# Six steps of the next row between one shift row's sum and its transposes, and three empty steps ahead of the first attention

## The chip, the cores and the metric

The kernel runs on one NeuronCore of a Trainium2 chip; nothing is shared with other cores. The metric is device time in microseconds (us) of one execution; the time before is the median of 3 runs. One more execution was profiled, and all rows of the trace come from it. TensorE (PE, with its weight loads PEld) multiplies matrices, VectorE (DVE) and ScalarE (ACT) do elementwise work, GpSimd (POOL) some small work and DMA issues, and SyncE (SP) issues most DMAs.

## The reference

One decoder block on x of 512 tokens and width 2048, in float32. The modulation comes from c (a vector of 2048): six vectors of 2048, shift, scale and gate for each half. Cut to what the change touches:

```
mod = silu(c) @ w_ada + b_ada            # shift1, scale1, gate1, shift2, scale2, gate2
h = rms_norm(x, norm1_w) * (1 + scale1) + shift1
aq, ak, av, gq, gf, gi, gg = split(h @ w_in)          # 7 parts of 1024 columns
attn = dilated_attention(rope(rms_norm(aq)), rope(rms_norm(ak)), av)   # 8 heads of 128
ho = hgrn2(gq, gf, gi, lb)               # f = lb + (1 - lb) * sigmoid(gf); 8 heads, chunked recurrence
...                                      # norms, silu(gg) gate, w_out, gate1, residual
x = x + gate2 * (square(relu(h2 @ w_ff1)) @ w_ff2)
```

The three branches of the dilated attention are merged by the weights of one masked softmax, so the kernel computes for each head the scores of 512 tokens against 512, one softmax and one product with the values.

## The kernel before

**Precision.** Each projection is made of three matmuls on parts in fp32r: a value is split into hi (a cast on ScalarE, L39) and lo (a subtraction on VectorE, L40), and hi x hi, hi x lo and lo x hi are summed in PSUM. `tok_mm` (L194, matmuls L198 to L200) puts tokens on partitions, `ch_mm` (L202, L206 to L208) puts channels there. The four buffers of each split tile (`whi`, `wlo`) let the splits run up to four k ahead of the matmuls.

**A projection.** `project` (L368) makes 512 columns: 16 steps of k (128 rows of the weight each), 12 matmuls of 128x128 by 128x512 in each, into four PSUM banks. The projections follow in this order: hv0 (values of the first half of HGRN heads), q0, k0, v0 (the first attention), `hgrn_q(1)` (L558, here hq1) and hv1, then q1, k1, v1 and two gate projections. Behind each, ScalarE copies the four banks out (`evac` L406, and L564 in `hgrn_q`). The next projection uses the same four banks, so its first matmuls wait for these copies.

**Two generators beside it.** Behind each k's matmuls, `project` calls `tick()` once, which takes one step of the first generator in `tasks` (HGRN heads, then attention, and so on), and then `bg_step()` as often as the rate says (2.0 for hv0, 1.85 for the others), which takes one step of the first generator in `bgw`, the background work. A step runs to the next `yield`. So the place of a `yield` decides behind which k an instruction stands on TensorE. From L835 on TensorE's instructions keep the order in which the program writes them (`manual_schedule`); the order on the other engines and the DMA queues is made by the tile framework's planner from its own model of times and priorities. `tc.high_priority()` marks what is to go first: weight loads and splits, the copies out of banks, and, with an offset of 400, the attention's softmax chain.

**The background rows.** A modulation or shift vector is a product of one vector with a matrix, and is made on VectorE: `gemv` (L116) loads one row block of 128 x 512 in each of 16 steps (SP's queue, L123) and multiplies and adds it to one of two accumulators (L127, L129). `to_cols` (L138) adds the two accumulators (the sum, L143), yields, and then lets TensorE transpose the result in four parts into one bank (L149), from which ScalarE sums each part into a column (L152). `mod_cols` makes such columns for the modulation, and `mod_rows` (L172) collects four of them, waits 3 steps, transposes the whole column into a bank `pr` (L180) and stores it to DRAM as gate1.

**Shift rows.** The first HGRN projections are made from h without shift1, and the shift's part is added afterwards: `shift_through(col0)` (L748) is `gemv` with the shift vector, `to_cols`, and then, for 4096, the forget gates of heads 0 to 3 (`forget`, L554: sigmoid on ScalarE, L555, and VectorE, L556), for 3072 the queries (L755 to L758). Its 18 steps are 16 rows, the sum, and the transposes with all that follows. Ahead of hv0 the background takes 76 steps: 72 of the four `shift_gen` and the first 4 of `shift_through(4096)`.

**HGRN heads.** `hgrn` takes 12 steps for each of four heads; a step mixes VectorE's products (`level`, L591) with small matmuls (`blocks32`, L577).

**Attention.** `attention` (L444) works on four heads: `heads_t(h)` transposes queries and keys (two banks, copied out by ScalarE at L456), `scores(h)` makes four matmuls into three banks (L468) and the softmax chain: VectorE's scale and mask (L474), maximum (L476, L477), ScalarE's exponential (L478). Four steps later `weights_t(h)` transposes the weights (three banks, L490, copied at L492), then `heads_t(h + 1)`, and in one step `values(h)` (one bank `po`, L501, divided and written by VectorE at L505) and `scores(h + 1)`. It has 25 steps. It is appended to `tasks` behind v0, and hgrn for the second half behind hv1.

**PSUM.** There are eight banks: four tagged "mm" for the projections and four tagged "bg" that everything else takes in turn.

Of the kernel before, what the change touches and what calls it, by code (L numbers as in the profile page):

```python
# [18 lines left out]
NK = D // P  # L19
# [25 lines left out]
def hybrid_block(ctx, tc, x, c, positions, norm1_w, w_ada, b_ada, w_in, q_norm_w, k_norm_w,  # L45
# [22 lines left out]
    def bank(name, tag="bg"):  # L68
        return ps.tile([P, 512], F32, name=name, tag=tag)
# [46 lines left out]
    def gemv(view, vec, col0, n=512, early=False):  # L116

        accs = [(work("acc") if early else gv.tile([P, 512], F32, name="acc"))[:, 0:n] for _ in range(2)]
        nk = 512 // n
        for k0 in range(0, NK, nk):  # L120
            raw = spare.pop(0) if early and spare else slot("araw") if early else gv.tile([P, 512], F32, name="araw", bufs=4)
            raw = raw.rearrange("p (k n) -> p k n", n=n)
            nc.sync.dma_start(raw, view[:, k0:k0 + nk, col0:col0 + n])  # L123
            for k in range(k0, k0 + nk):
                acc = accs[k % 2]
                if k < 2:
                    dve.tensor_scalar(acc, raw[:, k - k0], vec[:, k:k + 1], None, op0=ALU.mult)  # L127
                else:
                    dve.scalar_tensor_tensor(acc, raw[:, k - k0], vec[:, k:k + 1], acc, op0=ALU.mult, op1=ALU.add)  # L129
            yield  # L130
        gemv.acc = accs
# [6 lines left out]
    def to_cols(accs, dst):  # L138

        nb = accs[0].shape[1] // P  # L140
        parts = 1 if nb == 4 else 2
        if parts == 1:
            dve.tensor_tensor(accs[0], accs[0], accs[1], op=ALU.add)  # L143
        yield
        pc = bank("pc")
        for j in range(nb):
            for u in range(parts):
                c = (j * parts + u) * P
                pe.transpose(pc[:, c:c + P], accs[u][:, j * P:(j + 1) * P], ident)  # L149
        for j in range(nb):  # L150
            c = pc[:, j * parts * P:(j + 1) * parts * P]
            act.activation(c, c, AF.Copy, accum_out=dst[:, j:j + 1])  # L152
# [78 lines left out]
    def work(name, dt=F32):  # L231
        return wk.tile([P, 512], dt, name=name, tag="wk")
# [55 lines left out]
    def first_groups(c_f, c_q, before, after):  # L288

        bt = [bank("prj", tag="mm") for _ in range(4)]  # L290
        bc = [bank("prc") for _ in range(2)]
        for k0 in range(0, NK, 2):
            before(k0)
            wt = load_w(win_v, k0, c_f, ahead=False)
            wc = load_w(win_v, k0, c_q, 256, None, ahead=False)
            for j in range(2):
                k = k0 + j
                ch_mm(bt, hhi[k], hlo[k], *wt[j], k == 0, k == NK - 1)
                ch_mm(bc, hhi[k], hlo[k], *wc[j], k == 0, k == NK - 1)
            after(k0)  # L300
        return bt, bc
# [42 lines left out]
    bgw = []  # L344
# [9 lines left out]
    tasks = []  # L354
# [83 lines left out]
    def qk(c0, name, i):  # L438
        ts = evac(project(c0, tok_mm), name)
        rs = sm.tile([P, NT, 4], F32, name=f"rs{i}", bufs=2)  # L440
        bgw.insert(0, qk_norm(ts, i, rs))
        return ts if i else (ts, rs)

    def attention(qr, ks, vs):  # L444
        qs, rsq = qr

        place = {3: (0, 0), 2: (1, 0), 0: (1, 384), 1: (2, 0)}

        def heads_t(h):
            tT = []  # L450
            for i, src in enumerate((qs, ks)):
                pt = bank("ptq")
                for ti in range(NT):
                    pe.transpose(pt[:, ti * P:(ti + 1) * P], src[ti][:, h * DH:(h + 1) * DH], ident)
                t = work("qT")
                act.activation(t, pt, AF.Copy, scale=wcol[:, i:i + 1])  # L456
                tT.append(t)
            return tT

        def scores(h, qT, kT):  # L460
            lsum = sm.tile([P, NT], F32, name="lsum")
            m = sm.tile([P, NT], F32, name="m")
            ps_s = [bank("pscore") for _ in range(3)]
            s_sb = [work("s_sb") for _ in range(3)]
            for ti in (3, 2, 0, 1):
                n = (ti + 1) * P
                b, o = place[ti]
                pe.matmul(ps_s[b][:, o:o + n], lhsT=qT[:, ti * P:(ti + 1) * P], rhs=kT[:, 0:n], start=True, stop=True)  # L468
            for ti in (3, 2, 0, 1):
                n = (ti + 1) * P  # L470
                b, o = place[ti]
                s = s_sb[b][:, o:o + n]
                with tc.high_priority(offset=400):
                    dve.scalar_tensor_tensor(s, ps_s[b][:, o:o + n], rsq[:, ti, h:h + 1], lnc_sb[:, 512 - n:512],  # L474
                                             op0=ALU.mult, op1=ALU.add)
                    dve.tensor_reduce(m[:, ti:ti + 1], s, axis=AX.X, op=ALU.max)  # L476
                    dve.tensor_scalar(m[:, ti:ti + 1], m[:, ti:ti + 1], -1.0, None, op0=ALU.mult)  # L477
                    act.activation(s, s, AF.Exp, bias=m[:, ti:ti + 1], accum_out=lsum[:, ti:ti + 1])  # L478
            return s_sb, lsum

        def weights_t(s_sb):
            p_sb = []
            for b, tis in enumerate(((3,), (2, 0), (1,))):
                pT = bank("pT")
                p_sb.append(work("p_sb"))
                for ti in tis:
                    o = place[ti][1]
                    for sj in range(ti + 1):
                        c = slice(o + sj * P, o + (sj + 1) * P)
                        pe.transpose(pT[:, c], s_sb[b][:, c], ident)  # L490
                n = 256 if b == 2 else 512
                act.copy(p_sb[b][:, 0:n], pT[:, 0:n])  # L492
            return p_sb

        def values(h, p_sb, lsum):
            hs = slice(h * DH, (h + 1) * DH)
            po = bank("po")
            for ti in range(NT):
                b, o = place[ti]
                for sj in range(ti + 1):  # L500
                    pe.matmul(po[:, ti * P:(ti + 1) * P], lhsT=p_sb[b][:, o + sj * P:o + (sj + 1) * P],  # L501
                              rhs=vs[sj][:, hs], start=sj == 0, stop=sj == ti)
            dve.reciprocal(lsum, lsum)
            for ti in range(NT):
                dve.tensor_scalar(qs[ti][:, hs], po[:, ti * P:(ti + 1) * P], lsum[:, ti:ti + 1], None, op0=ALU.mult)  # L505

        tT = heads_t(0)
        yield
        p_sb = None
        for h in range(4):  # L510
            if h:
                values(h - 1, p_sb, lsum)
            s_sb, lsum = scores(h, *tT)
            for _ in range(4):
                yield
            p_sb = weights_t(s_sb)
            yield
            if h < 3:
                tT = heads_t(h + 1)
                yield  # L520
        values(3, p_sb, lsum)
        yield
# [31 lines left out]
    def forget(hd, src, f, bias=0.0):  # L554
        act.activation(f, src, AF.Sigmoid, bias=bias)  # L555
        dve.tensor_scalar(f, f, omlb[:, hd:hd + 1], lb[:, hd:hd + 1], op0=ALU.mult, op1=ALU.add)  # L556
# [191 lines left out]
    def shift_through(col0):  # L748

        yield from gemv(win_v, s1c, col0, early=col0 < 4096 + 512)  # L750
        col = sm.tile([P, 8], F32, name="scol", bufs=2)
        yield from to_cols(gemv.acc, col[:, 0:4])
        for h in range(4):
            if col0 == 3072:
                dve.tensor_scalar(col[:, 4 + h:5 + h], col[:, h:h + 1], QS, None, op0=ALU.mult)  # L755
                sg = wk.tile([P, 512], F32, name="sg", tag="ev", bufs=2)
                act.activation(sg, hq0[h], AF.Sigmoid, scale=1.0 / QS, bias=col[:, h:h + 1])
                dve.scalar_tensor_tensor(hq0[h], hq0[h], col[:, 4 + h:5 + h], sg, op0=ALU.add, op1=ALU.mult)  # L758
            else:
                f, hd = ((f0, h), (f1, 4 + h))[(col0 - 4096) // 512]  # L760
                forget(hd, f[h], f[h], col[:, h:h + 1])
        yield

    bgw += [shift_through(4096), shift_through(3072)]
    bt, bc = first_groups(4096, 3072, scale_block, shift_start)
    f0 = keep(bt, "f")
    hq0 = keep(bc, "gq", QS)
# [74 lines left out]
    q0 = qk(0, "aq", 0)  # L842
    k0_ = qk(1024, "ak", 1)
    v0 = evac(project(2048, tok_mm), "av")
    tasks.append(attention(q0, k0_, v0))
    hq1 = hgrn_q(1)
    hv1 = evac(project(5120 + 512, tok_mm), "gi")
    tasks.append(hgrn(f1, hq1, hv1, hrs[1]))
# [576 lines left out]
```

## Time and profile before

| | |
|---|---|
| median of 3 runs | 2282.14 us (2280.93 to 2285.49) |
| the profiled execution's own time | 2284.35 us |
| its span, first to last instruction | 2282.1 us |
| mean granted clock of TensorE | 0.996 of full speed |
| busy: PE, DVE, ACT, POOL | 97%, 79%, 48%, 19% of the span |
| moved by DMA | 598.31 MB, mean 262 GB/s |

Matmuls are pipelined: one that is shown with 390 ns starts about 230 ns behind the one before it, so the pace is read from the starts. A row of a timeline gives the start, the duration, the engine, the line, the operation with its output and inputs, the shape, the count, and in brackets the idle time of the engine before it with what ended it. A row of the waits gives the total, how often, and the longest. The clock column of a window is the share of full speed that TensorE was granted in it. What ended a wait is inferred from the semaphores' events.

### The profile page before, as it was taken

What the parts mean: (1) busy time and instruction counts of PE and PEld (TensorE: products, weight loads), DVE (VectorE), ACT (ScalarE), POOL (GpSimd) and SP (SyncE); (2) the same over time, 40 slices, a digit from 0 to 9 for tenths busy, and PEclk for the clock granted to TensorE, in tenths of its full rate; (3) what the DMA queues carried; (4) which work ended last, traced back from release to release, by engine and by line L of the source; (5) the groups of instructions that cost most, each with busy time, mean ns of one, the idle gap of its engine ahead of it and who ended that gap; (6) DMA issues with size and microseconds to landing.
All of it is one profiled execution on the core that took longest, in us unless ns stands there. A gap on an engine that the chain in (4) does not pass through costs nothing.

```text
span 2282.1 us, 33105 instructions
## 1 busy us (share of the span) xinstructions
PE 2224.0 (97%) x11769; PEld 1824.9 (80%) x11769; DVE 1809.7 (79%) x2765; ACT 1097.6 (48%) x1950; POOL 443.4 (19%) x664
## 2 busy tenths in 40 slices
PE   4899999999999999999999999999999999999999
PEld 3787877878778888888888888888888888888887
DVE  6999778668786575678658988988897679967878
ACT  5555344443444554547544555555564333443332
POOL 1000022000220000002232323323232222222221
PEclk9999999999999999999999999999999999999999
DMA  9799465546555256747979789889889987998884
GB/s 319 256 329 326 118 192 167 180 153 213 180 163 179 71 189 219 265 131 247 341 258 369 269 330 363 296 297 381 310 293 378 365 304 261 349 355 306 303 297 164
DMA packets 262582, 598.31 MB, mean 262 GB/s; under 512 B 23220, under 2 KB 43968, under 8 KB 262416
## 3 DMA queue, kind: packets, MB, share of 16 engines
q1 hardware_dynamic: 186800, 332.54, 43.3%
q0 software_dynamic: 70720, 254.21, 30.2%
q10 hardware_dynamic: 4896, 9.44, 1.2%
q8 instruction: 93, 1.52, 0.3%
q14 instruction: 73, 0.60, 0.1%
HBM read 518.49 MB, written 77.61 MB: 261 GB/s over the span
## 4 chain that ended last, share of the span: by engine, by line
PE 69%; issue 11%; DMA 11%; DVE 5%; POOL 3%; ACT 1%; SPq 0%; POOLq 0%; DVEq 0%; ACTq 0%
PE prj L198 9%; PE f L1183 9%; PE f L1182 9%; PE f L1181 9%; PE prj L200 9%; PE prj L199 9%; DMA f_lod<-fs 3%; PE f L208 2%; PE f L207 2%; PE f L206 2%; DMA araw<-in_w_ada_dram 2%; DMA araw<-in_w_in_dram 1%; DMA Fl<-f_lod 1%; DMA f_hid<-part 1%; PE prj L207 1%
## 5 line engine op out<-in xcount | busy, mean ns | idle before, releaser
L1165 ACT CAST vhi<-raw 128x1024 fp32r<-128x1024 f32 x392 | 413.4, 1055 | 533.9 <-PE f L1183 420.2
L1166 DVE TENSOR_TENSOR vlo<-raw,vhi 128x1024 fp32r<-128x1024 f32 x392 | 475.9, 1219 | 151.3 <-ACT vhi L1165 150.6
L1182 PE MATMUL f<-vlo,Fh 128*128 128x512 f32 x1376 | 537.0, 390 | 3.4 <-DVE vlo L1166 3.3
L1183 PE MATMUL f<-vhi,Fl 128*128 128x512 f32 x1376 | 535.7, 389 | 0.7 <-DMA Fl<-f_lod 0.7
L1181 PE MATMUL f<-vhi,Fh 128*128 128x512 f32 x1376 | 536.0, 390 | 0.0
L39 ACT CAST whi<-wraw 128x512 fp32r<-128x512 f32 (+1 forms) x368 | 220.0, 601 | 447.5 <-PE prj L200 309.2
L198 PE MATMUL prj<-whi,hi 128*128 128x512 f32 x896 | 365.1, 407 | 3.8 <-ACT gq L564 2.4
L200 PE MATMUL prj<-whi,lo 128*128 128x512 f32 x896 | 351.8, 393 | 0.0
L199 PE MATMUL prj<-wlo,hi 128*128 128x512 f32 x896 | 350.8, 392 | 0.0
L40 DVE TENSOR_TENSOR wlo<-wraw,whi 128x512 fp32r<-128x512 f32 (+1 forms) x368 | 242.4, 663 | 125.8 <-ACT whi L39 120.6
L129 DVE SCALAR_TENSOR_TENSOR acc<-araw,sc,acc 128x512 f32<-128x512 f32 (+1 forms) x392 | 253.2, 671 | 91.1 <-DMA araw<-in_w_ada_dram 90.0
L1182 PEld LDWEIGHTS f<-vlo,Fh 128*128 128x128 f32 x1376 | 258.3, 188 | 61.6 <-DVE vlo L1166 8.7
L1183 PEld LDWEIGHTS f<-vhi,Fl 128*128 128x128 f32 x1376 | 258.4, 188 | 55.0 <-DMA Fl<-f_lod 1.6
L1181 PEld LDWEIGHTS f<-vhi,Fh 128*128 128x128 f32 x1376 | 258.4, 188 | 53.4
L1149 DVE TENSOR_TENSOR raw<-raw,raw 128x1024 f32<-128x1024 f32 x224 | 268.0, 1217 | 3.3 <-DMA raw<-in_w_ff_dram 2.9
L198 PEld LDWEIGHTS prj<-whi,hi 128*128 128x128 f32 x896 | 169.3, 189 | 39.9 <-ACT gq L564 3.6
L200 PEld LDWEIGHTS prj<-whi,lo 128*128 128x128 f32 x896 | 168.9, 188 | 37.0 <-DVE lo L240 0.3
L199 PEld LDWEIGHTS prj<-wlo,hi 128*128 128x128 f32 x896 | 169.5, 189 | 32.4 <-DVE wlo L40 0.4
L1127 POOL DMA_DIRECT2D Fh<-f_hid x112 | 79.0, 705 | 425.8 <-PE f L1183 413.4
L208 PE MATMUL f<-hi,wlo 128*128 128x512 f32 x256 | 99.9, 390 | 1.9 <-DVE wlo L40 1.9
L206 PE MATMUL f<-hi,whi 128*128 128x512 f32 x256 | 100.3, 392 | 0.0
L207 PE MATMUL f<-lo,whi 128*128 128x512 f32 x256 | 99.6, 389 | 0.0
(311 smaller groups left out, 2913.1 us busy)
## 6 DMA issues: line engine op xcount, KB each, us to landing
raw<-in_w_ff_dram SPq DMA_DIRECT2D x224, 512.0 KB, 9.8
araw<-in_w_ada_dram SPq DMA_DIRECT2D x384, 256.0 KB, 4.3
Fh<-f_hid POOLq DMA_DIRECT2D x112, 512.0 KB, 6.7
Fl<-f_lod POOLq DMA_DIRECT2D x112, 512.0 KB, 7.9
wraw<-in_w_in_dram SPq DMA_DIRECT2D x104, 512.0 KB, 3.9
Fh<-h_hid POOLq DMA_DIRECT2D x60, 512.0 KB, 6.3
Fl<-h_lod POOLq DMA_DIRECT2D x60, 512.0 KB, 7.2
f_hid<-part POOLq DMA_DIRECT2D x48, 512.0 KB, 8.0
```

Of the source, the lines that this page charges most:

```text
L39: nc.scalar.copy(hi, src)
L40: (eng or nc.vector).tensor_tensor(lo, src, hi.bitcast(F32), op=ALU.subtract)
L129: dve.scalar_tensor_tensor(acc, raw[:, k - k0], vec[:, k:k + 1], acc, op0=ALU.mult, op1=ALU.add)
L198: pe.matmul(banks[ti], lhsT=hi[:, ts], rhs=whi, start=first, stop=False)
L199: pe.matmul(banks[ti], lhsT=hi[:, ts], rhs=wlo, start=False, stop=False)
L200: pe.matmul(banks[ti], lhsT=lo[:, ts], rhs=whi, start=False, stop=last)
L1149: dve.tensor_tensor(dst, a, b, op=ALU.subtract)
L1165: cast_done.append(act.copy(hi, src))
L1166: split_done.append(dve.tensor_tensor(lo, src, hi.bitcast(F32), op=ALU.subtract))
L1181: pe.matmul(banks[t], lhsT=fh[u][a][:, ts], rhs=whi[:, a], start=first, stop=False)
L1182: pe.matmul(banks[t], lhsT=fh[u][a][:, ts], rhs=wlo[:, a], start=False, stop=False)
L1183: pe.matmul(banks[t], lhsT=fl[u][a][:, ts], rhs=whi[:, a], start=False, stop=end)
```

## The change

Two things. The two shift rows 4096 (row a) and 3072 (row b) are no longer run one behind the other: `staggered` runs row a through its 16 rows and its sum (`NK + 1` steps), then six steps of row b, then what is left of a (its transposes and the forget gates), then the rest of b. The number of steps is the same. And `attention` gets an argument `lead`, the number of steps at its beginning in which it does nothing; the first attention gets 3, the second keeps 0.

```
-    def attention(qr, ks, vs):
+    def attention(qr, ks, vs, lead=0):
         qs, rsq = qr
...
+        for _ in range(lead):
+            yield
         tT = heads_t(0)
         yield
...
-    bgw += [shift_through(4096), shift_through(3072)]
+    def staggered(a, b, n_a, n_b):
+        for g, n in ((a, n_a), (b, n_b)):
+            for _ in range(n):
+                next(g)
+                yield
+        yield from a
+        yield from b
+
+    bgw.append(staggered(shift_through(4096), shift_through(3072), NK + 1, 6))
...
-    tasks.append(attention(q0, k0_, v0))
+    tasks.append(attention(q0, k0_, v0, 3))
```

## The prediction

> **What bounds the kernel now.** I read the page first, then the waits of TensorE, then the engines' timelines around the two places that the diff touches, then the windows of those places.
>
> ```profile
> span 2282.1 us, 33105 instructions
> ...
> PE 2224.0 (97%) x11769; PEld 1824.9 (80%) x11769; DVE 1809.7 (79%) x2765; ACT 1097.6 (48%) x1950; POOL 443.4 (19%) x664
> ```
>
> TensorE sets the time: it is busy 97% of the span. An edit that adds and removes no work can gain only what TensorE loses in waits, and what it loses by running slowly behind them. Its list of waits (who <- for what: us in all, times, longest) has three rows that matter here:
>
> ```profile
> PE pc L149 <- DVE acc L143: 4.8, 1, 4.8
> ...
> PE prj L198 <- ACT gq L564: 2.4, 2, 2.0
> ...
> PE prj L198 <- ACT gg L705: 1.3, 1, 1.3
> ```
>
> The first is the shift row's: the transposes of L149 wait once for the sum of L143. The second is at the seam between hgrn_q(1) and the projection behind it, under the first attention. The third is a seam under the second attention, which the diff leaves alone. TensorE's timeline (start, us, what, in brackets the idle time before it) shows the first:
>
> ```profile
> 207.57 0.39 PE L200 MATMUL prj<-whi,lo 128*128 128x512 f32 x1
> ...
> 210.29 0.39 PE L200 MATMUL prj<-whi,lo 128*128 128x512 f32 x1
> 215.53 1.12 PE L149 MATMUL pc<-ident,acc 128*128 128x128 f32 x4 [4.85 <-DVE acc L143]
> 216.30 0.78 PE L198 MATMUL prj<-whi,hi 128*128 128x512 f32 x1
> ...
> 220.29 0.47 PE L198 MATMUL prj<-whi,hi 128*128 128x512 f32 x1
> ...
> 242.87 0.60 PE L149 MATMUL pc<-ident,acc 128*128 128x128 f32 x4
> ```
>
> From 207.57 to 210.29 twelve matmuls start: 0.227 us from start to start, 2.72 us for the twelve of one k. TensorE would have started its transposes at 210.29 + 0.23 = 210.52 and did so at 215.53. Behind them nine matmuls, 216.30 to 220.29, take 0.443 each. The windows (length, busy us by engine, granted clock, DMA share, GB/s) tell why:
>
> ```profile
> 195.00:210.50 15.50, 15.50 (x72) 12.65 (x70) 14.86 (x25) 9.28 (x21) 0.53 (x1) 1.00 1.04 382
> 210.50:215.50 5.00, 0.18 (x1) 0.00 (x0) 5.00 (x10) 0.62 (x1) 0.00 (x0) 0.81 1.05 387
> 215.50:220.30 4.80, 4.77 (x14) 3.91 (x15) 4.41 (x8) 3.55 (x10) 0.00 (x0) 0.50 1.05 387
> 220.30:240.00 19.70, 19.70 (x88) 16.30 (x87) 15.16 (x27) 5.85 (x12) 0.00 (x0) 1.00 0.49 147
> ...
> 473.60:476.40 2.80, 2.80 (x7) 2.12 (x8) 1.46 (x4) 2.80 (x7) 0.00 (x0) 0.50 0.00 0
> ```
>
> The granted clock falls to 0.50 behind the wait and is 1.00 again at 220.3. So a wait of TensorE costs more than its own length. The seam, in the same timeline:
>
> ```profile
> 469.80 0.39 PE L208 MATMUL prj<-hi,wlo 128*128 128x512 f32 x1
> 472.14 0.50 PE L198 MATMUL prj<-whi,hi 128*128 128x512 f32 x1 [1.95 <-ACT gq L564]
> ...
> 473.60 0.79 PE L198 MATMUL prj<-whi,hi 128*128 128x512 f32 x1 [0.49 <-ACT gq L564]
> ...
> 476.33 0.46 PE L198 MATMUL prj<-whi,hi 128*128 128x512 f32 x1
> ```
>
> And ScalarE's side of it:
>
> ```profile
> 470.80 0.72 ACT L478 ACTIVATE s_sb<-s_sb,m 128x512 f32<-128x512 f32 x1 [2.90 <-DVE m L477]
> ...
> 471.53 0.56 ACT L564 COPY gq<-prj 128x512 f32<-128x512 f32 x1
> ...
> 475.46 0.58 ACT L564 COPY gq<-prj 128x512 f32<-128x512 f32 x1
> ```
>
> The copies that empty hgrn_q(1)'s four banks (L564) stand in ScalarE's queue behind an exponential of the attention, which waits 2.90 us for VectorE's maximum. The first copy starts 1.5 us after the last bank was filled (469.80 + 0.23), and exponentials stand between the four.
>
> **The change, part by part.** No instruction is added or removed.
>
> *The shift row.* In hv0's projection two background steps follow each k. Row a (4096) has taken 4 steps before it, so its 17th (the sum) and its 18th (transposes) both fall behind k 6. With six steps of row b between them the transposes fall behind k 9. Moved with them are 4 accumulating copies and 4 sigmoids on ScalarE and 4 operations of forget on VectorE. The rows' DMAs keep their order on SP (a's sixteen, then b's sixteen), since sum and transposes issue none; POOL's queue has nothing of either. Without the wait TensorE runs k 7 to 9 from 210.52 and reaches the transposes at 210.52 + 3 x 2.72 = 218.7. VectorE's rows:
>
> ```profile
> 211.13 0.68 DVE L40 TENSOR_TENSOR wlo<-wraw,whi 128x512 fp32r<-128x512 f32 x1
> ...
> 214.20 0.68 DVE L40 TENSOR_TENSOR wlo<-wraw,whi 128x512 fp32r<-128x512 f32 x1
> 214.80 0.68 DVE L143 TENSOR_TENSOR acc<-acc 128x512 f32<-128x512 f32 x1
> 215.40 0.68 DVE L40 TENSOR_TENSOR wlo<-wraw,whi 128x512 fp32r<-128x512 f32 x1
> ...
> 223.88 0.54 DVE L556 TENSOR_SCALAR f<-f,omlb,lb 128x512 f32<-128x512 f32 x1
> ...
> 225.00 0.69 DVE L40 TENSOR_TENSOR wlo<-wraw,whi 128x512 fp32r<-128x512 f32 x1
> ...
> 232.79 0.68 DVE L143 TENSOR_TENSOR acc<-acc 128x512 f32<-128x512 f32 x1
> ```
>
> The sum ends at 215.48, 3.2 us ahead of 218.7. What is late next? The three wlo of 211.13, 214.20 and 215.40 are those of k 8, 9 and 10 (whi has four buffers, so the cast of k+4 waits for the matmuls of k). TensorE needs them at 213.2, 216.0 and 219.1, and they end at 211.81, 214.88 and 216.08: all in time, the tightest by 1.1 us. The next one (225.00, k 11) would be 3.8 us too late for 221.9, but its cast stood behind the wait itself, as ScalarE's rows say:
>
> ```profile
> 221.81 0.60 ACT L39 CAST whi<-wraw 128x512 fp32r<-128x512 f32 x1
> 224.02 0.62 ACT L39 CAST whi<-wraw 128x512 fp32r<-128x512 f32 x1 [1.61 <-PE prj L200]
> ```
>
> These casts wait for TensorE, not for a transfer; k 7 now ends at 213.2, and the cast of k 11 can run then. The forgets end at 224.42, 8.9 us behind the transposes' start; from 218.7 that is 227.6, and row b's transposes, at hv0's end, now come at 242.87 - 7.3 = 235.6. Even the later sum of the timeline, 232.79, ends 2.1 us ahead of that. So this wait goes whole. Its worth needs the pace of four transposes without a wait, from a later stretch of TensorE's timeline:
>
> ```profile
> 352.24 0.66 PE L149 MATMUL pc<-ident,acc 128*128 128x128 f32 x4
> 352.65 0.47 PE L198 MATMUL prj<-whi,hi 128*128 128x512 f32 x1
> ```
>
> They take 0.41. From 210.52 the transposes and nine matmuls need 0.41 + 9 x 0.227 = 2.45 and would end at 212.97; they ended at 220.29. Gain 7.3.
>
> *The empty steps.* hgrn(0) has 48 steps and uses the 48 ticks of q0, k0 and v0, so the attention's first step falls behind k 0 of hgrn_q(1). Counted from there, the third head's scores fall behind k 13, and their exponentials on the seam. Three ticks later they fall behind k 0 of the next projection, which needs all four banks emptied; so they can't stand ahead of the copies any more. Around the seam stand instead the second head's weights_t (behind k 14) and the third's heads_t (behind k 15): copies that wait for TensorE alone, no VectorE chain. heads_t's eight transposes now lie between the last matmul of the one projection and the first of the next, and give the copies time. No DMA is in the attention, and its end, behind k 8 of hv1, moves to k 11 with four empty ticks left, so nothing behind it moves. Without the wait the nine matmuls from 472.14 on would start at 470.03 and be through at 470.03 + 9 x 0.227 = 472.07, not 476.33. Gain 4.3.
>
> *A new wait.* Counting on, the second head's values and scores now fall behind k 10, and in the same k the background transposes gate1's column (pr, L180), which stood alone there before. po and the scores take all four background banks, so pr must have po's, and TensorE's queue stands until VectorE's L505 has read it; behind it wait the matmuls of k 11. The nearest pairs, TensorE's scores and VectorE's L505:
>
> ```profile
> 438.77 2.32 PE L468 MATMUL pscore<-qT 128*128 128x512 f32 x8
> ...
> 462.38 2.32 PE L468 MATMUL pscore<-qT 128*128 128x512 f32 x8
> ```
>
> ```profile
> 438.97 1.13 DVE L505 TENSOR_SCALAR aq<-po,lsum 128x128 f32<-128x128 f32 x4 [1.11 <-PE po L501]
> ...
> 464.04 1.12 DVE L505 TENSOR_SCALAR aq<-po,lsum 128x128 f32<-128x128 f32 x4
> ```
>
> L505 ends 1.0 ahead of the scores' end in the first and 0.5 behind it in the second. So the cost is 0 (no gain is possible in a new wait) to 0.5; if VectorE's queue happens to stand at a row that has not landed, up to 5.1:
>
> ```profile
> DVE acc L129 <- DMA araw<-in_w_ada_dram: 90.0, 74, 5.1
> ```
>
> I take 0.5, from the nearest row. SP's store of the gate row waits as much longer, and the row loads behind it; they feed only background work.
>
> *Sum.* 7.3 + 4.3 - 0.5 = 11.1. The profiled execution took 2284.35 (span 2282.1 and 2.25 around it), so 2273.25 on its scale. It lies 2.21 above the median of the runs, so I predict 2282.14 - 11.1 = **2271.0**.
>
> **One rule on the clock.** The row 473.60:476.40 has the clock at 0.50 behind a wait of 1.95 and one of 0.49. [...]
>
> **The rivals.**
> *A wlo behind the forgets.* VectorE works its queue in order. The cast of k 13 is released by k 9's end, the very moment of the new transposes; if its wlo is queued behind the four forgets, as 225.00 is behind 223.88, it ends 225.69 - 215.53 = 10.2 behind the transposes' start, and TensorE wants it after 0.41 + 3 x 2.72 = 8.6. That is a wait of 1.6 and, at the seam's rate (4.3 for 2.4 of waiting), 1.8 of slow clock: 2274.4. For it: that order stands in the trace. Against: weight splits have high priority. 12%.
> *The seam keeps a wait.* Other ScalarE work (weights_t, heads_t, the tanh of gq) holds the copies as long: 2271.0 + 4.3 = 2275.3. For it: ScalarE is busy 2.80 of 2.80 in 473.60:476.40. Against: none of it waits for VectorE ahead of the copies. 12%.
> *The transfers are the bound.* From 195.0 to 220.3 the DMA share is 1.04 to 1.05 at 382 to 387 GB/s. If weights come no earlier, TensorE waits for them instead, the first gain is lost: 2271.0 + 7.3 = 2278.3, within 0.2%. Against: the casts' waits end on TensorE, and from 220.3 the share is 0.49. 5%. [...]
> *Slower: a re-made order of VectorE in q0 to v0.* All engines but TensorE are ordered anew by the planner from the diff on. hgrn's ladder alternates TensorE and VectorE at every tick; if VectorE starts it with the backlog of later forgets, a rung comes late. Each such wait, at the seam's size, costs 4.3. Two give 2279.6, three 2283.9, and from four on it is slower: 2288.2. Against it, VectorE waits for TensorE in the ladder, not the reverse:
>
> ```profile
> 256.40 0.29 DVE L618 TENSOR_TENSOR mt<-pA,hgm 128x128 f32<-128x128 f32 x1 [1.57 <-PE pA L577]
> ```
>
> Two or three 9%, four or more 8%.
> That the change doesn't do what it says would need the planner to move TensorE's instructions; it keeps their written order here, so that has no share of its own.
>
> **How the numbers follow.** The forecast has 54%. 0.2% is 4.6 us, about what a measurement can tell. Faster by more: forecast, first and second rival, 78%. Within: transfers 5% and two or three late rungs 9%, 14%. Slower: 8%. Range: below, the new wait at 0 (2270.5), the runs' spread of 1.2 under their median, and the 1.3 of the second attention's seam if a new order happens to take it: 2268.0. Above, up to the transfers' case: 2278.5. That holds 83%.
>
> **What would show it.** Right: the L143 row gone from TensorE's waits, or under 1 us; no half clock near 215; L564 gone from them; the matmuls at the seam 0.227 apart; pr behind the scores with at most 0.5 of idle. Wrong: a wait for wlo (L40) in hv0, a wait for gq or qT at the seam, waits at L577, or a DMA as releaser of a cast. The prediction falls if TensorE's waits between 200 and 500 still come to more than 3 us in all.

## The result, and the profile after

| | before | after |
|---|---|---|
| median of 5 runs each, one chip | 2282.23 us (2280.93 to 2287.92) | 2274.34 us (2274.03 to 2275.7) |
| ratio after to before, 95% interval | | 0.996 (0.9949 to 0.9972) |
| the profiled execution's own time | 2284.35 us | 2275.3 us |
| its span | 2282.1 us | 2273.6 us |

The change makes the kernel faster by 7.9 us in the medians, and by 6.4 to 11.6 us by the interval of the ratio; the forecast was 11.1 us, from 2282.14 to 2271.0. The measured time lies inside the forecast range of 2268.0 to 2278.5. Ratios use the runs within 1.5% of a kernel's fastest, and one run in all lies outside that, of e8_both_leads with 5777.86 us. The busy row of the page of after:

```profile
PE 2222.2 (98%) x11769; PEld 1824.7 (80%) x11769; DVE 1809.1 (80%) x2765; ACT 1096.9 (48%) x1950; POOL 442.2 (19%) x664
```

The counts behind the five engines are those of before: the work is the same, and the span is 8.5 us shorter. TensorE's list of waits, cut to 200 to 500 us:

```profile
PE pr L180 <- DVE aq L505: 2.3, 1, 2.3
PE pc L149 <- DVE acc L143: 0.3, 1, 0.3
```

Before, this stretch held 4.8 for L143 and 2.4 for gq. The first is down to 0.3, the second is gone (the copies stand at L566 now, two lines further down), and a wait of 2.3 at pr is new. TensorE's timeline at the shift row and at row b's transposes:

```profile
218.00 0.39 PE L200 MATMUL prj<-whi,lo 128*128 128x512 f32 x1
218.23 0.60 PE L149 MATMUL pc<-ident,acc 128*128 128x128 f32 x4
218.58 0.48 PE L198 MATMUL prj<-whi,hi 128*128 128x512 f32 x1
...
235.47 0.66 PE L149 MATMUL pc<-ident,acc 128*128 128x128 f32 x4 [0.28 <-DVE acc L143]
```

Row a's transposes follow the matmul before them at its pace. The windows of the stage:

```profile
210.00:220.00 10.00, 10.00 (x47) 8.28 (x47) 10.00 (x18) 3.39 (x9) 0.00 (x0) 1.00 1.05 387
```

TensorE is busy for 10.00 of 10.00 us at full clock, where before it stood for 4.85 us and then ran at 0.50. VectorE's timeline of the stage (the forgets stand at L558 now):

```profile
214.34 0.68 DVE L143 TENSOR_TENSOR acc<-acc 128x512 f32<-128x512 f32 x1
...
219.80 0.68 DVE L40 TENSOR_TENSOR wlo<-wraw,whi 128x512 fp32r<-128x512 f32 x1
...
221.80 0.55 DVE L558 TENSOR_SCALAR f<-f,omlb,lb 128x512 f32<-128x512 f32 x1
...
225.68 0.68 DVE L40 TENSOR_TENSOR wlo<-wraw,whi 128x512 fp32r<-128x512 f32 x1
...
234.73 0.68 DVE L143 TENSOR_TENSOR acc<-acc 128x512 f32<-128x512 f32 x1
```

The sum of row a ends at 215.02, 3.2 us ahead of the transposes. Row b's sum ends at 235.41, and that is the 0.28. At the seam behind hgrn_q(1), TensorE and then ScalarE:

```profile
460.88 0.40 PE L208 MATMUL prj<-hi,wlo 128*128 128x512 f32 x1
461.12 0.60 PE L454 MATMUL ptq<-ident,aq 128*128 128x128 f32 x4
461.56 0.60 PE L454 MATMUL ptq<-ident,ak 128*128 128x128 f32 x4
461.91 0.48 PE L198 MATMUL prj<-whi,hi 128*128 128x512 f32 x1
```

```profile
459.24 0.59 ACT L566 COPY gq<-prj 128x512 f32<-128x512 f32 x1
...
460.39 1.06 ACT L566 COPY gq<-prj 128x512 f32<-128x512 f32 x2
...
462.39 0.59 ACT L566 COPY gq<-prj 128x512 f32<-128x512 f32 x1
...
471.49 0.72 ACT L478 ACTIVATE s_sb<-s_sb,m 128x512 f32<-128x512 f32 x1 [5.81 <-DVE m L477]
```

The third head's queries and keys (eight transposes, L454) lie between the projections, no matmul waits for the copies, and the exponential that stood among them comes 9 us behind the last of them. Now the new wait, TensorE first:

```profile
437.80 2.39 PE L501 MATMUL po<-av,p_sb 128*128 128x128 f32 x20
440.03 2.32 PE L468 MATMUL pscore<-qT 128*128 128x512 f32 x8
444.62 0.28 PE L180 MATMUL pr<-ident,gcol 128*16 128x128 f32 x1 [2.27 <-DVE aq L505]
```

```profile
442.77 0.75 DVE L129 SCALAR_TENSOR_TENSOR acc<-araw,sc,acc 128x512 f32<-128x512 f32 x1 [1.47 <-DMA araw<-in_w_ada_dram]
443.44 1.12 DVE L505 TENSOR_SCALAR aq<-po,lsum 128x128 f32<-128x128 f32 x4
```

VectorE had nothing to do for 1.47 us, though po was filled: at the head of its queue stood a background row (L129) that had not landed, and the division of po (L505) stood behind it. The chain that ended last, in order of time, says the same from the other end:

```profile
438.12 4.55 DMA araw<-in_w_ada_dram
...
442.77 0.63 DVE acc L129
...
443.44 0.61 DVE aq L505 x3
...
444.62 0.28 PE pr L180
```

A load that serves only background work is on the path here, because two queues lie between it and the matmuls, and each was worked in order here: VectorE's, idle for 1.47 us ahead of the row with L505 behind it, and TensorE's, idle for 2.27 us at pr with k 11 behind it.

### The profile page after: what moved, and what is told of

Read it like the earlier page. It is cut to its first block, busy times and chain, and to the rows that moved or that the text cites. A ratio compares the mean times of both kernels' runs of the same rounds, so it can differ in the third digit from the quotient of the medians.

```text
span 2273.6 us, 33111 instructions
## 1 busy us (share of the span) xinstructions
PE 2222.2 (98%) x11769; PEld 1824.7 (80%) x11769; DVE 1809.1 (80%) x2765; ACT 1096.9 (48%) x1950; POOL 442.2 (19%) x664
## 4 chain that ended last, share of the span: by engine, by line
PE 76%; DVE 8%; DMA 7%; issue 6%; ACT 2%; POOL 1%; SPq 0%; POOLq 0%; DVEq 0%; ACTq 0%
PE f L1192 10%; PE f L1193 10%; PE f L1191 10%; PE prj L198 9%; PE prj L200 9%; PE prj L199 9%; DVE vlo L1176 2%; PE f L208 2%; PE f L206 2%; PE f L207 2%; PE prj L206 2%; PE prj L207 2%; PE prj L208 2%; DVE raw L1159 2%; DMA f_lod<-fs 1%
## 5 line engine op out<-in xcount | busy, mean ns | idle before, releaser
L198 PE MATMUL prj<-whi,hi 128*128 128x512 f32 x896 | 363.6, 406 | 1.3 <-ACT gg L707 1.3
L129 DVE SCALAR_TENSOR_TENSOR acc<-araw,sc,acc 128x512 f32<-128x512 f32 (+1 forms) x392 | 253.8, 673 | 98.6 <-DMA araw<-in_w_ada_dram 97.7
L198 PEld LDWEIGHTS prj<-whi,hi 128*128 128x128 f32 x896 | 168.3, 188 | 36.2 <-ACT gg L707 1.6
```

Source lines behind the costliest of these rows:

```text
L198: pe.matmul(banks[ti], lhsT=hi[:, ts], rhs=whi, start=first, stop=False)
```

## The experiments

Ratios are to the kernel before, run beside it on the same chip. The traces are compared at three anchors of TensorE's timeline, which are the same matmul in each kernel; a difference between two anchors is the worth of what lies between them, free of how the beginning went. They are the first `pA` of hgrn(0), hq1's first matmul, and one L198 behind hv1's end; in before and in after, anchor by anchor:

```profile
248.87 0.46 PE L577 MATMUL pA<-gq,kk 128*32 128x32 f32 x32
...
409.55 0.47 PE L206 MATMUL prj<-hi,whi 128*128 128x512 f32 x1
...
528.02 0.39 PE L198 MATMUL prj<-whi,hi 128*128 128x512 f32 x1
```

```profile
241.53 0.46 PE L579 MATMUL pA<-gq,kk 128*32 128x32 f32 x32
...
402.21 0.47 PE L206 MATMUL prj<-hi,whi 128*128 128x512 f32 x1
...
520.06 0.39 PE L198 MATMUL prj<-whi,hi 128*128 128x512 f32 x1
```

After is 7.34 ahead at the first two and 7.96 at the third. Of the 7.34, 0.38 is there already at hv0's first matmul (188.76 in before, 188.38 in after). So row a gave about 7.0, and seam and pr together only 0.6. The theory from here on: the seam is worth what was forecast, and pr's wait takes it back, because a row that has not landed stands at the head of VectorE's queue. Rivals: the seam was never worth 4; or pr waits for something else than that row.

### Each part alone

**e1_steps_only**: the six steps without the empty ones.

```
-    tasks.append(attention(q0, k0_, v0, 3))
+    tasks.append(attention(q0, k0_, v0))
```

> The six steps of row b alone, no empty steps. Theory (three waits that add up: row a's sum 7.3, the seam 4.3, pr behind the scores -4.3): row a's wait is gone, the seam's wait of about 2.4 with its slow clock stays, pr stands alone and waits for nothing; 2282.2 - 7.3 = 2274.9, so as fast as the whole change. Rival (the shortfall is spread over a re-made order, not one wait): the gain differs from 7.3 by more than 1.5, and small waits are found elsewhere.

Measured: 2278.41 us (2274.64 to 2279.36, 6 runs) beside 2284.75 (17 runs), ratio 0.9969 (0.9956 to 0.9981), 7.1 us by the ratio. The seam's wait is there as before, pr's is not; TensorE's waits between 200 and 800:

```profile
PE prj L198 <- ACT gq L566: 2.7, 2, 2.5
PE pc L149 <- DVE acc L143: 0.3, 1, 0.3
```

The first part does by itself what was forecast for it, and the new wait belongs to the second.

**e2_lead_only**: the empty steps without the six.

```
-    bgw.append(staggered(shift_through(4096), shift_through(3072), NK + 1, 6))
+    bgw += [shift_through(4096), shift_through(3072)]
```

> The three empty steps alone, rows a and b one behind the other as before. Theory: the seam's 4.3 is gained and the same 4.3 is lost behind pr; no change, 2282.2 with 1 us either way, with row a's wait of 4.85 in the trace and a wait of pr for L505 of about 2.3. Rival (pr's wait is a chance of the shifted times of the changed kernel and would be 0 to 0.5 here): 2278.

Measured: 2280.43 us (2276.64 to 2283.02, 12 runs), ratio 0.998 (0.9972 to 0.9988): 4.6 us faster by the ratio, not 0. That is a miss. Its waits between 200 and 800:

```profile
PE pc L149 <- DVE acc L143: 4.9, 1, 4.9
PE pr L180 <- DVE aq L505: 1.8, 1, 1.8
...
```

Row a's wait and pr's are there and the seam's is gone, as expected. What the expectation had wrong is the price: in the profiled execution no slow clock followed pr's 1.79 us (the clock is 1.00 from 448.80 to 453.00), and from hq1's start to hv1's end this kernel gains 2.65 us against before, which is about the seam's 4.6 (below) less 1.8. The same happened in part to row a: 4.85 us of waiting were followed by 3.41 us at half clock (214.02 to 217.43) instead of before's 6.83. The last section sets these stretches side by side.

### What holds TensorE at pr

**e3_pr_early**: the whole change, with pr one step earlier and one more empty step behind it, so that pr does not stand behind po and the scores.

```
-    def mod_rows(kind, dst, lag=3):
+    def mod_rows(kind, dst, lag=3, rest=0):
...
-        yield
+        for _ in range(1 + rest):
+            yield
...
-    later.append(mod_rows(2, gate1))
+    later.append(mod_rows(2, gate1, 2, 1))
```

> The change with pr one step earlier (it falls behind k 9, after heads_t, whose banks are free) and one step more behind it, so that all later background steps stay. Theory: pr no longer needs po's bank, its wait of 2.27 and the slow clock behind it go: 2274.3 - 4.3 = 2270.0. Rival (pr's wait hides another one that is late just as well, or the slow clock comes anyway): 2272.5 to 2274.3.

Measured: 2271.38 us (2270.14 to 2273.17, 5 runs), ratio 0.994 (0.9928 to 0.9953). From hq1's start to hv1's end it gains 4.6 us against before, after gained 0.6: the seam is worth 4.6, and pr took 4.0 of it. VectorE around the division, which stands at L506 in this kernel:

```profile
442.51 0.75 DVE L129 SCALAR_TENSOR_TENSOR acc<-araw,sc,acc 128x512 f32<-128x512 f32 x1 [1.10 <-DMA araw<-in_w_ada_dram]
443.18 1.12 DVE L506 TENSOR_SCALAR aq<-po,lsum 128x128 f32<-128x128 f32 x4
```

```profile
439.79 2.32 PE L469 MATMUL pscore<-qT 128*128 128x512 f32 x8
441.76 0.59 PE L207 MATMUL prj<-hi,whi 128*128 128x512 f32 x1
```

The division comes as late as in after, behind the same kind of row, and TensorE goes straight on: nothing in its queue needs po's bank. So the late division costs nothing by itself; pr's place does.

**e4_row_behind**: pr stays where the change has it, but of the `gemv` rows that the program writes behind the first division, VectorE may not start those from k 10 on before that division.

```
+                    with tc.issue_after(held[0].ins) if held and k >= 10 else ExitStack():
+                        dve.scalar_tensor_tensor(acc, raw[:, k - k0], vec[:, k:k + 1], acc, op0=ALU.mult, op1=ALU.add)
...
+                last = dve.tensor_scalar(qs[ti][:, hs], po[:, ti * P:(ti + 1) * P], lsum[:, ti:ti + 1], None, op0=ALU.mult)
+            held.append(last)
```

> The change with pr where it is, but VectorE's rows from the 11th on of each vector are ordered behind the first L505. Theory: L505 was late because a row whose load had not landed stood ahead of it in VectorE's queue; L505 now runs when po is done and pr waits 0 to 0.5: 2270.0 to 2271.0. Rival (L505 is late by VectorE's own work or by po itself): pr still waits 2 us, 2274.3.

Measured: 2271.51 us (2269.55 to 2278.34, 6 runs), ratio 0.9945 (0.9929 to 0.9961). TensorE and VectorE (its lines are three further down):

```profile
439.74 2.32 PE L471 MATMUL pscore<-qT 128*128 128x512 f32 x8
441.89 0.27 PE L183 MATMUL pr<-ident,gcol 128*16 128x128 f32 x1
```

```profile
439.94 1.12 DVE L508 TENSOR_SCALAR aq<-po,lsum 128x128 f32<-128x128 f32 x4 [1.12 <-PE po L504]
440.98 1.41 DVE L132 SCALAR_TENSOR_TENSOR acc<-araw,sc,acc 128x512 f32<-128x512 f32 x2
```

With the rows behind it the division is ready when po is, and pr, in the change's own place, follows the scores without a wait. From hq1's start to hv1's end it gains 4.6 us against before, as e3 does. The two remove the wait from its two ends, the order on VectorE and the order on TensorE, and both bring 4.0 us there: the cause is shown. What the wait costs an execution on average is taken up further down.

### The two sizes

**e5_two_steps** (e3 with two steps of row b instead of six: `NK + 1, 2`).

> The kernel with pr early, and two steps of row b between row a's sum and its transposes instead of six: the transposes fall behind k 7 instead of k 9, 5.4 us earlier. Theory: they come 2.2 us ahead of the sum's end (218.2 - 5.4 = 212.8 against 215.0), so a wait of 2.2 for the sum is back; with no slow clock it costs 2.2 against the kernel with pr early, with one slow window behind it up to 3.9: 9 to 11 faster than before. Rival (the planner moves the sum along with its reader, so that the distance doesn't matter): no wait, 12.5 faster than before.

Measured: 2275.45 us (2272.96 to 2277.77, 6 runs) beside 2282.75 (16 runs), ratio 0.9967 (0.9955 to 0.9979), 7.5 us faster by the ratio; expected were 9 to 11, so the time is a miss. TensorE at row a:

```profile
213.77 0.87 PE L149 MATMUL pc<-ident,acc 128*128 128x128 f32 x4 [2.13 <-DVE acc L143]
```

The wait itself came as the counting has it, one k of 2.72 us shorter than before's 4.85; it still drew 3.41 us at half clock (214.07 to 217.48). In the profiled execution the price is as expected: from hv0's first matmul to the first `pA` e5 takes 3.4 us longer than e3. The six times lie in two groups, near 2273 and near 2277.5, and the profiled one is in the lower; what the upper three paid, no trace shows.

**e6_two_empty** and **e7_four_empty**: the change as it is, with 2 or 4 empty steps instead of 3.

> The change with two empty steps instead of three, pr where it was. The third head's values and scores now fall behind k 15, right on the seam, and pr falls one k behind the second head's scores. Theory: the copies out of the banks are ready before these scores, so no exponential is ahead of them, and L505 has a whole k (2.7 us) before pr; neither wait: 11.6 to 12.5 faster than before. Rival (what counts is the distance of the scores from the seam, as the waits of before suggest): exponentials stand among the copies again, a wait of gq of 2 us or more at the seam, 8 faster.

> The change with four empty steps. pr falls behind heads_t of the second head (two free banks), weights_t of the second head on the seam. Theory: no wait of pr and none at the seam: 11.6 to 12.5 faster than before. Rival (the three weight copies of ScalarE on the seam hold the copies out of the banks): a wait of gq of about 1.3, 10 faster.

Measured: 2273.45 us (2269.49 to 2275.98, 5 runs), ratio 0.9956 (0.9944 to 0.9969), and 2272.34 us (2270.93 to 2277.78, 5 runs), ratio 0.996 (0.9947 to 0.9972). In both traces TensorE waits between 200 and 800 only for L143 (0.3) and, at the output projection, for gg (1.3); spans 2269.8 and 2269.6. Both clear the seam, and in both pr falls behind another k than values and scores. So of the three sizes only the one chosen puts pr in the k of po and the scores. The mechanism is as expected, and from hq1's start to hv1's end the two gain 4.5 and 4.2 us; the times fall short of the 11.6 to 12.5 expected, with 10.0 and 9.1 us by the ratios, and their lead over the change, if they have one, is within the runs' spread.

### The second attention

The trace of before has a third wait at a seam, 1.3 for gg. **e8_both_leads** is e3 with three empty steps at the second attention too:

```
-    tasks.append(attention(q1, k1, v1))
+    tasks.append(attention(q1, k1, v1, 3))
```

> pr early, and three empty steps ahead of the second attention as well. Theory: the seam under the second attention (a wait of 1.33 for gg) is the same mechanism and goes; nothing in that stage stands where pr did: 1.3 faster than pr early, 13.8 faster than before. Rival (the seam's wait comes from the work on gg itself, or the later end of the attention holds up the norm behind it): same as pr early, 12.5, or slower.

Measured: 2281.48 us (11 runs, ten of them 2278.72 to 2285.45) beside 2282.75 (16 runs), ratio 0.9993 (0.9984 to 1.0002), which is a miss: about 12 us slower than e3 by the ratios, not 1.3 faster. The gg wait is gone; in its place, in TensorE's list:

```profile
PE prj L199 <- ACT hi L240: 4.5, 2, 3.0
...
PE prj L201 <- DVE lo L241: 3.5, 2, 2.9
```

The waits lie from 796 to 810 us, where the output projection begins, and two stretches at half clock follow (a mean of 0.53 from 800.40 to 804.00 and of 0.59 from 810.00 to 814.20). By the program the second attention's last head feeds that projection, through the norm and the splits, so it has no slack as the first has; that is the rival's case, the later end. One of the four waits, of 2.9 us, has the mechanism of pr besides: the split it waits for (L241, at 809.49) stands on VectorE behind background rows that waited for their loads (L127 and L129, from 805.07, 807.25 and 808.82 on), while the casts ahead of it ran at 805.90. The four waits come to 8.0 us, less the 1.3 that went, and half of twice 3.41, the length of after's slow stretch, makes by estimate 6.7 + 3.4 = 10.1; from hv1's end to a matmul behind all four e8 takes 10.4 longer than e3 (312.3 against 301.9). The gg wait is not, as the prediction says, at a seam under the second attention: it is at 811.42 in before, at the seam between the last gate projection and the output projection.

### How often pr's wait comes

The profile shows one execution, so the change and e3 were run beside each other twice more.

> The changed kernel itself, beside the next one on the same chip. Theory: 7.5 to 8.5 faster than before, and 4 slower than the kernel with pr early, by the one wait of pr for L505; the trace shows that wait again, of about 2.3.

> The kernel with pr early, beside the changed kernel on the same chip. Theory: 4 faster than the changed kernel (12 faster than before). Rival (the difference so far was that of two chips): within 1 of the changed kernel.

> The change as it is, beside the next kernel once more, to tell how often pr's wait takes its full price. Theory: the wait for the row that has not landed comes in nearly every execution, with its half clock; then this kernel stands 3 to 5 us above the one with the early pr, in the medians too. Rival: the row's landing varies, and in many executions the wait is short or draws no half clock; then the two medians lie within 1.5 us, and the traces alone differ, each showing one execution.

> The change with pr two steps earlier, once more beside the change. Theory: 3 to 5 us under the change in the medians, no wait of TensorE between 236 and 798 us in the trace. Rival: within 1.5 us of the change in the medians, with the same trace.

| | the change | pr early (e3's kernel) |
|---|---|---|
| e9, e10 | 2272.75 (2272.15 to 2278.75), 0.9964 (0.9952 to 0.9976) | 2272.2 (2270.79 to 2279.93), 0.9962 (0.9948 to 0.9975) |
| e11, e12 | 2276.28 (2272.26 to 2277.28), 0.9963 (0.9951 to 0.9976) | 2272.55 (2269.43 to 2273.19), 0.9949 (0.9935 to 0.9963) |

All three traces of the change have the wait (2.27, 2.81 and 2.71 us) with slow clock behind it: 3.41 us at 0.50 in after (445.47 to 448.88) and in e9 (444.15 to 447.56), and in e11 matmuls about 0.43 us from start to start from 444.33 to 446.87, where 0.23 follows. None of the three of pr early has it (e12's kernel is e3's, with pr one step earlier; between 236 and 798 us its trace has one other wait, of 0.5 for z at L679). From hq1's start to hv1's end the three of the change gain 0.6, 0.3 and 0.3 us against before, the three of pr early 4.6 each: in the executions that were profiled the wait costs 4.0 to 4.3 us. In the medians pr early lies 0.55 and 3.7 us lower, the first as the rivals had it, the second as the theories; over both pairs together it is 2272.55 (11 runs) against 2275.40 (10 runs). The profiled execution of e9 took 2278.75 us, its four others 2272.15 to 2274.58. Whole times are a blunt measure here, for the 14 profiled executions reach hv0's first matmul anywhere between 185.57 and 188.76 us. How much of the wait an execution without a profile pays on average is not settled between 0.5 and 4 us, and the intervals of the ratios overlap.

## Why the prediction was right, and where it was not

**Row a: right in mechanism and size.** Forecast 7.3 us, transposes without a wait at 218.7, the sum at 215.48. Measured: 218.23 and 215.02, both early by about the 0.38 us by which this execution was ahead at hv0's beginning; 7.0 us from hv0's first matmul to the first `pA`, and 7.2 with row b's new 0.28 added back. Ten of the eleven traces with the six steps give 6.9 to 7.0 there, e9's 6.7. That 0.28 is a small miss: the prediction checked row b's transposes against the sum's place in before, 232.79, and VectorE's new order put it at 234.73.

**The seam: right.** Forecast 4.3 us; e3 and e4 show 4.6 each from hq1's start to hv1's end. The mechanism is that of the text: ScalarE's copies no longer stand behind an exponential, and eight transposes give them time.

**pr: the mechanism was named, its size was not.** This is the step that failed: "I take 0.5, from the nearest row." Measured were 2.27 us of waiting and, behind it, 3.41 us at half clock; between the anchors 4.0 us. With 4.0 in its place the sum is 7.3 + 4.3 - 4.0 = 7.6, and from hv0's first matmul to hv1's end the trace gains 7.6; that the medians' 7.9 lies so near is in part luck, as executions differ by up to 3 us in their beginnings alone. Two things were wrong with the 0.5. The first of the two pairs that it was read from had no background row ahead of the division, but the second, which gave the 0.5, had one that waited for its load. In before:

```profile
462.77 0.75 DVE L129 SCALAR_TENSOR_TENSOR acc<-araw,sc,acc 128x512 f32<-128x512 f32 x1 [0.50 <-DMA araw<-in_w_ada_dram]
```

Behind this row and one split came L505 at 464.04, though po's matmuls were through by 462.54. So the nearest row held the very mechanism, with a load that was not late by much; the case of a later one was given with its price, up to 5.1, and put aside as chance. And the 0.5 to 5.1 were the wait alone, though the prediction had charged slow clock to both other waits. (It also calls values and scores both the second head's; the values are the first head's.)

**The rivals.** A wlo behind the forgets: the split of k 13 ran at 219.80, ahead of the first forget at 221.80; that of k 14 stood behind them, at 225.68, with 3 us to spare. (The price of this rival is also added up wrongly: at the rate it names, 4.3 for 2.4, a wait of 1.6 comes to 2.9, not 3.4.) The seam keeping a wait: no. The transfers as the bound: the DMA share stayed at 1.05 and 387 GB/s in the stage and the wait still went, so that share did not bound TensorE. Late rungs in the ladder: the list of waits between 200 and 500 has no row for L579. Of what the prediction said would show it wrong nothing came, and its bound of 3 us of waiting between 200 and 500 held with 2.6, nearly all of it at pr; but of its signs of being right one failed, the idle of at most 0.5 at pr.

## What to carry to other kernels

When a change moves an instruction behind one that shares its rotating buffer, its price depends, as here, on what stands ahead of the releasing instruction in that engine's queue; look there for an operation that waits for a load, also in the rows that you take a size from. Here TensorE waits of 1.95 us (the seam in before) and 2.13 us (row a in e5) drew slow clock and pr's of 1.79 us in e2 did not, so look at the granted clock behind a wait and count that in beside its length. Delaying a generator is free only where its end has slack, as e8 shows: look at what its last step feeds.

## What the runs showed of the hardware

A wait's slow clock looked like chance: 4.85 us drew 6.83 us at half clock in before and 3.41 in e2; pr's wait drew 3.41 or none. Two regularities of these traces go with it. First, up to TensorE's last matmul the half-clock stretches start at 94.17, 213.64 and 473.05 in before and last 6.83, 6.83 and 3.41 us; in after they start at 52.94, 93.90 and 445.47 and last 3.41, 6.83 and 3.41. The starts lie 35 and 76 times 3.413 us apart in before, 12 and 103 times in after, so within each of the two executions they lie on one grid. Second, the stretches go with how busy TensorE was in the cell of that grid ahead of them. The cells around the waits (length, busy PE, PEld, DVE, ACT and POOL, clock, DMA share, GB/s), in before for row a and the seam, in after for pr, in e2 for pr:

```profile
210.23:213.64 3.41, 0.45 (x3) 0.03 (x1) 3.41 (x7) 0.62 (x1) 0.00 (x0) 1.00 1.05 387
213.64:217.06 3.42, 1.53 (x6) 1.43 (x7) 3.42 (x6) 0.37 (x2) 0.00 (x0) 0.50 1.06 388
469.64:473.05 3.41, 1.46 (x6) 0.61 (x4) 1.91 (x9) 2.25 (x8) 0.00 (x0) 1.00 0.00 0
```

```profile
442.06:445.47 3.41, 1.14 (x7) 0.72 (x6) 2.70 (x7) 0.26 (x1) 0.00 (x0) 1.00 0.73 251
445.47:448.88 3.41, 3.41 (x10) 2.64 (x9) 3.41 (x8) 0.00 (x0) 0.00 (x0) 0.50 0.59 166
```

```profile
446.13:449.54 3.41, 1.62 (x9) 1.04 (x8) 2.55 (x7) 0.26 (x1) 0.00 (x0) 1.00 0.66 210
```

A cell in which TensorE was busy for 0.45, 1.14 or 1.46 of 3.41 us is followed by one at half clock; one with 1.62 is not. The cells at e1's seam (0.93), at row a in e5 (1.28) and at pr in e9 (1.12) are followed by slow ones too. In before and after, from 40 us on, every cell at full clock with TensorE busy for 1.44 us or less was followed by a slow one, and none with 1.80 or more; with 1.46 both occur, in before at 469.64, with a slow cell behind it, and at 49.80, with a fast one. A slow cell that was itself busy for 1.53 (row a's in before), 2.50 (before, 94.17) or 2.71 us (after, 93.90) was followed by another; those busy for 2.92 (before, 473.05) and 3.41 us (after, 52.94 and 445.47) ended the stretch. In e2 row a's wait fell into two cells, busy for 1.73 us (207.19 to 210.61, no slow cell behind it) and 0.25 us (210.61 to 214.02, just ahead of the wait's end), so the slow cell was full, 3.41 us, and the only one.

As an estimate from these cells, a wait cost its length and half the busy time of the slow cells: at pr 2.27 + 3.41 / 2 = 4.0, as between the anchors; for row a 4.85 + (1.53 + 3.41) / 2 = 7.3, where the anchors gave 7.0, or 7.2 with row b's 0.28; for pr in e9, whose slow cell is busy for 2.88 us, 2.81 + 1.44 = 4.3, as the anchors gave; for the seam 1.95 + 0.49 + 2.92 / 2 = 3.9, where they gave 4.6. It is also no more than an estimate from them that a wait of some 2 us shared by two cells, each still busy for 1.80 us or more, would cost its length alone, so that a shift of the kernel by a microsecond or two could add or remove 1.7 us (half of 3.41) at an unrelated wait: no run here moved a wait across the grid on purpose.
